# A hybrid decoder step on one core: sampled tokens' state space steps run in stages, the first norm ahead of the first weight, the residual behind the last head, convolution states beside z4 to z7

## The chip, the cores and the metric

The kernel runs on one core of a Trainium2 chip. Its time is the device time of one execution in microseconds (us); lower is better. A core has five engines with a queue each: TensorE (PE; PEld is its weight load), VectorE (DVE), ScalarE (ACT), GpSimd (POOL) and SyncE (SP). SP issues nearly all DMAs of this kernel, in order, from one queue. Every engine executes its own instructions in order; semaphores order them across engines.

## The reference

One layer of a decoder for 1024 prompt positions and 8 sampled tokens (1032 columns together, `NT`). After an RMSNorm one projection `w_in` feeds two mixers, and their outputs, each normed and gated, go through `w_out` and are added to the input; a gated MLP with a short convolution follows.

```python
h = rmsnorm(x, w['norm1_w'])
proj = h @ w['w_in']
q_r, f_r, i_r, g_r, z, xbc_r, dt_r = jnp.split(proj, splits, axis=-1)
...
o_a, S_h_new = hgrn2_mix(heads(q), heads(k), heads(i_r), heads(log_f), S_h)      # 8 heads
o_a = rmsnorm(o_a, w['hgrn_norm_w']) * jax.nn.silu(heads(g_r))
...
xbc, buf_s_new = causal_dwconv(xbc_r, buf_s, w['ssm_conv_w'], w['ssm_conv_b'])
xs, Bm, Cm = jnp.split(jax.nn.silu(xbc), [D_SSM, D_SSM + SSM_GROUPS * SSM_STATE], axis=-1)
y, S_s_new = ssd_scan(X * dt[..., None], A * dt, Bh, Ch, S_s)                    # 16 heads, 2 groups
y = (y + w['ssm_d'][:, None] * X).reshape(Bsz, L, D_SSM) * jax.nn.silu(z)
y = rmsnorm(y.reshape(Bsz, L, SSM_GROUPS, -1), ...)
...
x = x + jnp.concatenate([o_a, y], axis=-1) @ w['w_out']
```

For a sampled token the scan is one step: its state (64 x 128 per head, read from and written to memory) is decayed, gets `x * dt` times `B` added, and is multiplied by `C` and summed. This is the decode step below. New convolution states are outputs as well.

## The kernel before

Activations lie transposed: 128 features on the partitions, 1032 columns. Each fp32 product is made of three TensorE products of halves, high by high, low by high and high by low (`hh`, `hl` for activations; `wh`, `wl` for weights, rounded on ScalarE at L190 and subtracted on VectorE at L192). A projection job (`x0`, `z4`, `q3` ...) loads 512 KB of `w_in` and runs 3 chunks of 344 columns, 24 matmuls each, and evicts each chunk.

The order of the work on TensorE is written by hand. The list `jobs` holds the projections in order: the convolved inputs, z0 to z3, f, q, v, sg of head 0, z4 to z7, those of head 1 and on, and then `o8.0`, `o8.2`, `o12.0`, `o12.2`, `o8.4`, `o8.6`, `o12.4`, `o12.6` (the half of `w_out` for state space outputs, two blocks of 128 output rows each), and later the other half, the up and the down projection. `drive` runs the matmuls of these jobs between those of a chain: the state space scan of group 0, that of group 1, and the heads one after another, so that TensorE has work while the chain waits for VectorE. Smaller pieces hang on the count of job matmuls: `after(n, work)` runs `work` n of them later, and `spread` runs a generator's pieces so far apart. On the other engines a scheduler places the instructions by the order of issue and by the buffers, and it may draw an instruction ahead.

A decode step, `ssm_decode(g, i)`, treats 128 rows (two heads) for all 8 tokens in two halves of four tokens. Each half fetches the state `Sd` (256 KB) and the broadcast `Bb` and `Cb` (256 KB each), scales `Sd` on ScalarE in four instructions (L641), multiplies `Bb` (L642) and adds it (L643) on VectorE, stores the state, multiplies by `Cb` on GpSimd (L645) and reduces on VectorE (L646). It runs whole where it is called: group 0 at x5, x7, z0 and z1, beside the first scan, group 1 at z4 to z7. Its result goes into the 8 sampled columns of the same tile as the prompt's, and the gate and the norm (`ssm_gate`) work on all 1032 columns.

In a scan, `ssd_front` makes `bg`, `bt`, `xp`, `xdt` and the decays `csb`, `ssd_back` the products `yo`, `st`, `yd`, the new state `S` (L583) and the sums in `ecs` and `xbc`; `sT` transposes the last `S`. In a head, `vd` and `vtp` transpose v, `a` is the intra-chunk product, `ktp`, `kt` and `kv` make the chunk states, `o` the output, `dms` and `hms` the sums for its norm. Transposes to be done now and then (`vd`, `dms`, the convolution states' `cst`, the residual's `xtd`) share a PSUM tag, "nx", with a single buffer.

The residual: `token_blocks` copies the prompt in blocks to `xb_d`; `residual_load` fetches two 256 KB tiles `xs` for each of the eight row blocks m, and `residual` transposes them on VectorE in 32 x 32 blocks (L806), adds them on GpSimd (L803), and adds the sampled columns from a TensorE transpose `xtd` (L810, L811). It hangs on the o8 jobs; `o8.0` and `o8.2` run beside the last head.

At the start `first_norm` norms three tiles of 128 tokens (L112 to L118), then transposes them (`tp`) into `hh` and `hl`; the first two weights are loaded and rounded before.

Of the kernel before, what the change touches and what calls it, by code (L numbers as in the profile page):

```python
# [12 lines left out]
ALU = mybir.AluOpType  # L13
# [37 lines left out]
def hybrid_layer(  # L51
# [54 lines left out]
    def first_norm(tiles):  # L106
        xs = []
        for i in tiles:
            xt, t0, n = xtm[i]
            xn = [half("xn"), half("xn")]  # L110
            ss = keep.tile([P, 4], F32, tag="ss", bufs=4, name=nm("ss"))
            for i in range(2):  # L112
                A.activation(xn[i][:n], xt[:n, i * 512:(i + 1) * 512], AF.Square, accum_out=ss[:n, i:i + 1])
            V.tensor_tensor(ss[:n, 2:3], ss[:n, 0:1], ss[:n, 1:2], op=ALU.add)
            A.activation(ss[:n, 3:4], ss[:n, 2:3], AF.Sqrt, bias=epsc[:n], scale=1.0 / DM)
            V.reciprocal(ss[:n, 3:4], ss[:n, 3:4])
            for i in range(2):
                V.tensor_scalar(xn[i][:n], xt[:n, i * 512:(i + 1) * 512], ss[:n, 3:4], None, op0=ALU.mult)  # L118
            xs.append((xn, t0, n))
        c0, c1 = xs[0][1], xs[-1][1] + xs[-1][2]  # L120
        for k in range(KT):
            tp = bank("tp")
            for xn, t0, n in xs:
                PE.transpose(tp[:, t0 - c0:t0 - c0 + n], xn[k // 4][:n, (k % 4) * P:(k % 4 + 1) * P], ident[:n, :n])
            A.activation(hT_hi[k][:, c0:c1], tp[:, :c1 - c0], AF.Copy, scale=col("n1", k))
            V.scalar_tensor_tensor(hT_lo[k][:, c0:c1], tp[:, :c1 - c0], col("n1", k),
                                   hT_hi[k][:, c0:c1].bitcast(F32), op0=ALU.mult, op1=ALU.subtract)
# [52 lines left out]
    def wload(src, kt, m=P, kept=None):  # L180
# [9 lines left out]
        A.copy(wh[:, :n], ws[:, :n])  # L190
        if not again:
            V.tensor_tensor(wl[:, :n], ws[:, :n], wh[:, :n].bitcast(F32), op=ALU.subtract)  # L192
        if kept is not None:
            if again:
                SP.dma_start(wl.bitcast(F32), wl_d[kept[0]])
            else:
                SP.dma_start(wl_d[kept[0]], wl.bitcast(F32))
        return (wh[:, :n].rearrange("p (k m) -> p k m", m=m), wl[:, :n].rearrange("p (k m) -> p k m", m=m))
# [163 lines left out]

    def xbc_close(j, ext):
# [5 lines left out]
        A.activation(acc[:, :T], acc[:, :T], AF.Silu)  # L369
        A.activation(acc[:, T:NT], acc[:, T + 3:T + 32:4], AF.Silu)  # L370
# [21 lines left out]
    first = [(j, wload(w_in_[0, :, OFF_X + j * P:OFF_X + (j + 1) * P], KT), xbc_open()) for j in (8, 10)]  # L392
    for i in range(3, 9):
        load_x(i)
    vec_cols(0)
    for c in range(NCH):
# [29 lines left out]
    G.memset(dtr[:, :NT], 0.0)  # L426
# [98 lines left out]
    for g in range(4):  # L525
        rows = slice(32 * g, 32 * g + 32)
        V.tensor_copy(mlow[rows], lowf[rows, :, rows])
        V.tensor_copy(eyec[rows], ident[rows, rows])
# [99 lines left out]
    def ssm_decode(g, i):  # L628
        j = g * 4 + i
        xdd = small.tile([P, 2, ND], F32, tag="xdd", name=nm("xdd"))  # L630
        xdec = Xg[g][i][:, T:NT]
        V.tensor_tensor(xdd[:, 0, :], xdec, ddb[:, 0, j, :], op=ALU.mult)
        for b0 in (0, 4):
            bs = slice(b0, b0 + 4)
            Bb, Cb = tl("d", "Bb")[:, :512], tl("d", "Cb")[:, :512]
            for t_, r in ((Bb, 2 * g), (Cb, 2 * g + 1)):
                fetch(t_, bc_d[r, bs].rearrange("b n -> (b n)").unsqueeze(0).to_broadcast([P, 512]))
            Sd = tl("ld", "Sd")
            fetch(d4(Sd), state_ssm[0, bs, 2 * j:2 * j + 2].rearrange("b h p n -> (h p) b n"))
            for b in range(4):  # L640
                A.activation(d4(Sd)[:, b, :], d4(Sd)[:, b, :], AF.Copy, scale=ddb[:, 1, j, b0 + b:b0 + b + 1])  # L641
            V.tensor_tensor(d4(Bb), d4(Bb), cb(xdd[:, 0, bs]), op=ALU.mult)  # L642
            V.tensor_tensor(Sd, Sd, Bb, op=ALU.add)  # L643
            SP.dma_start(ssm_sample[0, bs, 2 * j:2 * j + 2].rearrange("b h p n -> (h p) b n"), d4(Sd))
            G.tensor_tensor(Cb, Sd, Cb, op=ALU.mult)  # L645
            V.tensor_reduce(xdd[:, 1, bs], d4(Cb), axis=mybir.AxisListType.X, op=ALU.add)  # L646
        V.scalar_tensor_tensor(xdec, xdec, d_bc[:, j:j + 1], xdd[:, 1, :], op0=ALU.mult, op1=ALU.add)

    def rstd_of(dst, tmp, ps, n):
# [6 lines left out]
    gr_d = dram.tile([2, 4, QW], F32, name="gr_d")  # L656

    def ssm_gate(g):
        acc = []

        def z_job(i):
            j = g * 4 + i

            def begin():
                if i == 0:
                    acc.append(tl("g", "gacc"))
                if g:
                    ssm_decode(1, i)
                elif i < 2:
                    ssm_decode(0, i + 2)  # L670

            def evict(c, cs, ps):
                Y = Xg[g][i][:, cs]
                sz = tl("z", "sz")[:, :CH]
                A.activation(sz, ps, AF.Silu)
                V.tensor_tensor(Y, Y, sz, op=ALU.mult)
# [9 lines left out]
        def rstd():  # L686
            ps = bank("ms", "nx")
            for q in range(4):
                mm(ps[32 * q:32 * q + 32, :QW], ones[:, 0:32], acc[0][:, q * QW:(q + 1) * QW])
            nt = tl("z", "nt")  # L690
            rstd_of(nt[:, :QW], tl("z", "nt")[:, :QW], ps[:, :QW], 512)
            SP.dma_start(gr_d[g], nt[::32, :QW])
            after(36, rows)

        def rows():
            fetch(acc[0][:, :NT], gr_d[g].rearrange("a t -> (a t)").unsqueeze(0).to_broadcast([P, NT]))
            after(20, lambda: spread(tail(), 6))

        def tail():
            for i in range(4):  # L700
                j = g * 4 + i
                Y = Xg[g][i][:, :NT]
                V.scalar_tensor_tensor(Y, Y, col("sn", j), acc[0][:, :NT], op0=ALU.mult, op1=ALU.mult)
                SP.dma_start(mix_d[8 + j], Y)
# [63 lines left out]
    G.memset(am, 0.0)  # L768
# [3 lines left out]
    V.tensor_tensor(selod, ident[:, 0:ND], ident[:, 32:32 + ND], op=ALU.add)  # L772
# [9 lines left out]

    def token_blocks():
        for m in range(KT):
            for a in range(4):
# [3 lines left out]
                yield  # L789

    def residual_load(m):
        ms = slice(m * P, (m + 1) * P)
        xs = [tl("d", "xs")[:, :512] for _ in range(2)]
        xd = small.tile([ND, P], F32, tag="xd", name=nm("xd"))
        for i in range(2):
            fetch(xs[i], xb_d[m][:, i * 512:(i + 1) * 512])
        fetch(xd, x_sample[:, 0, ms])
        return xs, xd

    def residual(out, xs, xd):  # L800
# [4 lines left out]
        for i0 in range(2):  # L805
            V.transpose(xs[i0], xs[i0])  # L806
            if i0 == 0:
                add(out[0][:, 0:512], xs[0])
                ps = bank("xtd", "nx")
                PE.transpose(ps[:, :ND], xd, ident[:ND, :ND])  # L810
                V.tensor_tensor(out[1][:, 508:516], out[1][:, 508:516], ps[:, :ND], op=ALU.add)  # L811
# [7 lines left out]
    def head_in(h):  # L819
# [8 lines left out]
        for n, off, func in (("f", OFF_F, AF.Tanh), ("q", OFF_Q, AF.Silu), ("v", OFF_I, AF.Copy),  # L828
# [4 lines left out]
            def begin(n=n):  # L833
                t[n] = tl("e" if h == 0 and n == "f" else "big", n)
# [218 lines left out]
    def out_job(r0, m, halves=(0, 1), last=False):  # L1053
        def load():
            w = wload(w_out[0, r0 * P:(r0 + 4) * P, m * P:(m + 2) * P], 4, 2 * P,
                      kept=(r0 // 4 * 4 + m // 2, halves[0]) if len(halves) == 1 else None)
            return w, [residual_load(m + i) for i in range(2)] if r0 == 8 else None

        def run(loads):
# [4 lines left out]
            if res:  # L1064
# [4 lines left out]
            for i in range(2):  # L1069
                for hf in halves:  # L1070
                    for c in range(2):
# [4 lines left out]
                        if res:  # L1076
# [8 lines left out]
                if res:  # L1085
                    spread(residual([xh[hf][m + i] for hf in range(2)], *res[i]), 8)
# [432 lines left out]
```

## Time and profile before

| | |
|---|---|
| median of 3 runs | 1765.24 us (1763.6 to 1767.99) |
| the profiled execution | 1764.89 us, its span 1763.2 us |
| mean granted TensorE clock | 0.995 |
| busy: PE, DVE, ACT, POOL | 1709.8, 1097.8, 778.7, 478.8 us |
| DMA queue of SP | 197.68 MB, 37.0% of 16 engines' span |

A row of a timeline gives start and duration in us, engine, line, operation, output and inputs, shape and count, and in brackets how long the engine idled before it and what released it. A row of waits gives the waiting engine and line, the releaser, the total in us, how often, and the longest. In a row of the windows the length of the window comes first, then busy us (and number of instructions) by engine, then the granted clock of TensorE (1.00 is full speed), the DMA share and GB/s.

### The profile page before, as it was taken

The page shows a single profiled execution, that of the slowest core. Times are in us where ns is not written, and L with a number is a line of the kernel's source. Part 1 is how long each engine was busy: PE and PEld are TensorE (multiplying, and loading weights), DVE is VectorE, ACT ScalarE, POOL GpSimd, SP SyncE. Part 2 cuts the span into 40 slices and gives each one's busy share as a digit, 9 for nine tenths or more (in the row PEclk, how much of TensorE's full clock was granted, in tenths as well). Part 3 has the DMA queues.
Part 4 walks back from the last instruction along what each step waited for, and adds up shares of the span by engine and source line. Part 5 has one row for each costly group of instructions (what it writes and reads, how often), then busy time and mean ns, then how long its engine had stood idle before and what let it go on. Part 6 is the DMA issues. An engine that isn't in the chain of part 4 may idle for free. (4 is left out here: it accounts for less than half of the span.)

```text
span 1763.2 us, 38543 instructions
## 1 busy us (share of the span) xinstructions
PE 1709.8 (97%) x16115; PEld 1659.4 (94%) x16115; DVE 1097.8 (62%) x1978; ACT 778.7 (44%) x1422; POOL 478.8 (27%) x485
## 2 busy tenths in 40 slices
PE   7999899999999999999799999999999999999998
PEld 6998789899999999999799989999999999999997
DVE  6668966566554554566636687776667767445545
ACT  7577686444434344344423374343333434111114
POOL 2103231111110110111220355666666664000002
PEclk9999999999999999999999999999999999999999
DMA  5355644553232332234336832222222226422312
GB/s 166 65 148 149 173 120 143 167 169 120 83 93 57 98 87 72 77 110 144 114 115 210 250 123 73 73 85 82 88 73 73 79 82 214 153 83 78 98 61 97
DMA packets 250132, 200.23 MB, mean 114 GB/s; under 512 B 47252, under 2 KB 220870, under 8 KB 249942
## 3 DMA queue, kind: packets, MB, share of 16 engines
q1 hardware_dynamic: 249670, 197.68, 37.0%
q8 instruction: 126, 2.06, 0.5%
q14 instruction: 48, 0.39, 0.1%
q0 software_dynamic: 288, 0.10, 0.0%
HBM read 155.17 MB, written 46.95 MB: 115 GB/s over the span
## 5 line engine op out<-in xcount | busy, mean ns | idle before, releaser
L93 PE MATMUL mm<-hl,wh 128*128 128x344 f32 x1248 | 406.1, 326 | 0.0
L93 PE MATMUL mm<-hh,wh 128*128 128x344 f32 x1248 | 405.6, 326 | 0.0
L93 PE MATMUL mm<-hh,wl 128*128 128x344 f32 x1248 | 402.8, 323 | 0.8 <-issue 0.8
L93 PEld LDWEIGHTS mm<-hl,wh 128*128 128x128 f32 x1248 | 236.1, 189 | 4.8 <-issue 4.2
L93 PEld LDWEIGHTS mm<-hh,wh 128*128 128x128 f32 x1248 | 236.1, 189 | 4.2 <-issue 3.4
L93 PEld LDWEIGHTS mm<-hh,wl 128*128 128x128 f32 x1248 | 236.3, 189 | 1.4 <-issue 1.2
L190 ACT CAST wh<-ws 128x1024 fp32r<-128x1024 f32 x96 | 100.6, 1048 | 254.9 <-PE dn L93 134.9
L93 PE MATMUL ub<-uh,wh 128*128 128x258 f32 x704 | 199.5, 283 | 4.2 <-DVE fext L1332 2.7
L93 PE MATMUL ub<-uh,wl 128*128 128x258 f32 x704 | 198.7, 282 | 0.0
L93 PE MATMUL ub<-ul,wh 128*128 128x258 f32 x704 | 198.6, 282 | 0.0
L93 PE MATMUL dn<-ah,wh 128*128 128x256 f32 (+1 forms) x640 | 181.1, 283 | 2.0 <-DVE x L1449 2.0
L93 PE MATMUL dn<-al,wh 128*128 128x256 f32 (+1 forms) x640 | 180.6, 282 | 0.0
L93 PE MATMUL dn<-ah,wl 128*128 128x256 f32 (+1 forms) x640 | 180.1, 281 | 0.0
L192 DVE TENSOR_TENSOR wl<-ws,wh 128x1024 fp32r<-128x1024 f32 x88 | 108.8, 1236 | 78.5 <-ACT wh L190 77.7
L93 PE MATMUL ua<-uh,wh 128*128 128x258 f32 x528 | 149.3, 283 | 1.5 <-DVE val L1344 1.3
L93 PE MATMUL mm<-mh,wh 128*128 128x258 f32 x512 | 146.9, 287 | 3.0 <-ACT x L1077 1.8
L93 PE MATMUL ua<-ul,wh 128*128 128x258 f32 x528 | 149.1, 282 | 0.0
L93 PE MATMUL ua<-uh,wl 128*128 128x258 f32 x528 | 148.4, 281 | 0.0
L93 PE MATMUL mm<-ml,wh 128*128 128x258 f32 x512 | 145.4, 284 | 0.9 <-DVE ml L1037 0.9
L93 PE MATMUL mm<-mh,wl 128*128 128x258 f32 x512 | 145.2, 284 | 0.0
L93 PEld LDWEIGHTS ub<-uh,wh 128*128 128x128 f32 x704 | 133.0, 189 | 4.9 <-DVE fext L1332 2.9
L1282 DVE TENSOR_TENSOR wl<-wt,wh 128x512 fp32r<-128x512 f32 x88 | 89.1, 1031 | 73.8 <-ACT wh L1281 73.8
(353 smaller groups left out, 3981.9 us busy)
## 6 DMA issues: line engine op xcount, KB each, us to landing
ws<-in_w_in_dram SPq DMA_DIRECT2D x52, 512.0 KB
ws<-in_w_up_dram SPq DMA_DIRECT2D x44, 512.0 KB
ws<-in_w_out_dram SPq DMA_DIRECT2D x24, 512.0 KB
act_d<-val SPq DMA_DIRECT2D x22, 516.0 KB
al<-act_d SPq DMA_DIRECT2D x22, 516.0 KB
ws<-in_w_down_dram SPq DMA_DIRECT2D x22, 512.0 KB
ml<-mix_d SPq DMA_DIRECT2D x48, 172.0 KB
csb<-cs_d SPq DMA_DIRECT2D x32, 256.0 KB
```

The source lines that it names most:

```text
L93: PE.matmul(out, lhsT, rhs, start=start, stop=stop)
L190: A.copy(wh[:, :n], ws[:, :n])
L192: V.tensor_tensor(wl[:, :n], ws[:, :n], wh[:, :n].bitcast(F32), op=ALU.subtract)
L1282: V.tensor_tensor(lo[:, cs], sums[name], hi[:, cs].bitcast(F32), op=ALU.subtract)
```

## The change

- *Start.* `wload` can hold back the rounding of a weight. The first weight's is issued behind the third tile's norm, the second's behind the first `hh` and `hl`; two GpSimd memsets and some small copies on VectorE wait until the third norm is done.
- *Decode steps.* Each is split into stages hung on the job count: fetches at once, the products of the first half 36 matmuls later, of the second 56, the first sum 64, the second 84. Group 0 starts at sg of head 0 and at z4, z5, z6, group 1 at v of heads 2 to 5 (that is, while the chains of heads 1 to 4 run). The sampled columns get tiles of their own, `xdk` and `szd`, and a gate and a norm of their own, with a sum on TensorE, `dgs`, in the "nx" bank. The prompt's norm covers 1024 columns.
- *Convolution states* move from beside heads 1 to 3 to z4 to z7, a piece each 24 matmuls instead of 60, and the token blocks follow 260 matmuls after.
- *Residual.* Blocks 0 to 3 go with `o8.4` and `o8.6`, 4 to 7 with `o12.4` and `o12.6`, none with `o8.0` and `o8.2`. The sampled tokens are transposed once, eight transposes in one bank copied to `xsT`.

```diff
+    def first_rounded():
+        with tc.issue_after(early[0].ins), tc.issue_after(early[1].ins):
+            held[0]()
+        behind.append(early[0].ins)
...
-        first_norm(range(3 * c, 3 * c + 3))
+        first_norm(range(3 * c, 3 * c + 3), *((None, None) if c else (first_rounded, held[1])))
...
-            if j in (5, 7):
-                ssm_decode(0, (5, 7).index(j))
...
-        xdec = Xg[g][i][:, T:NT]
+        xdec = xdk[:, j, :]
...
+        def front(bs, Bb, Cb, Sd):
             for b in range(4):
-                A.activation(d4(Sd)[:, b, :], d4(Sd)[:, b, :], AF.Copy, scale=ddb[:, 1, j, b0 + b:b0 + b + 1])
+                A.activation(d4(Sd)[:, b, :], d4(Sd)[:, b, :], AF.Copy, scale=ddb[:, 1, j, bs.start + b:bs.start + b + 1])
             V.tensor_tensor(d4(Bb), d4(Bb), cb(xdd[:, 0, bs]), op=ALU.mult)
             V.tensor_tensor(Sd, Sd, Bb, op=ALU.add)
...
+        after(36, lambda: front(*got[0]))
+        after(56, lambda: front(*got[1]))
+        after(64, lambda: back(*got[0]))
+        after(84, end)
...
+    def decode_norm(g, js, dg):
+        ps = bank("dgs", "nx")
+        mm(ps[:, :ND], ones, dg[:, 4, :])
+        rstd_of(dg[:, 4, :], dg[:, 5, :], ps[:, :ND], 512)
...
-                if g:
-                    ssm_decode(1, i)
-                elif i < 2:
-                    ssm_decode(0, i + 2)
+                if g and i < 3:
+                    ssm_decode(0, i + 1)
...
+            if m == 0:
+                ps = bank("xtd", "nx")
+                for k in range(KT):
+                    PE.transpose(ps[:, k * ND:(k + 1) * ND], xs[k // 4][:ND, blk[k % 4]], ident[:ND, :ND])
+                V.tensor_copy(xsT, ps[:, :KT * ND].rearrange("p (k b) -> p k b", b=ND))
...
-                ps = bank("xtd", "nx")
-                PE.transpose(ps[:, :ND], xd, ident[:ND, :ND])
-                V.tensor_tensor(out[1][:, 508:516], out[1][:, 508:516], ps[:, :ND], op=ALU.add)
+                add(out[1][:, 508:516], xsT[:, m, :])
...
+                if h == 0 and n == "sg":
+                    ssm_decode(0, 0)
+                elif 2 <= h <= 5 and n == "v":
+                    ssm_decode(1, h - 2)
...
-            return w, [residual_load(m + i) for i in range(2)] if r0 == 8 else None
+            rm = {(8, 4): 0, (8, 6): 2, (12, 4): 4, (12, 6): 6}.get((r0, m))
+            return w, [(rm + i, residual_load(rm + i)) for i in range(2)] if rm is not None else []
...
+    job("conv", None, once(lambda: spread(conv_states(), 24, lambda: after(260, lambda: spread(token_blocks(), 30)))))
     ssm_gate(1)
     heads[1] = head_in(1)
-    job("conv", None, once(lambda: spread(conv_states(), 60, lambda: spread(token_blocks(), 40))))
```

How the instructions move, at three places. First VectorE's queue in the first scan, around the state `S` of its third chunk. Before (`Sd`, `Cb` and `xdd` belong to a decode step, the rest to the scan):

```order
L643 TENSOR_TENSOR Sd_1696<-Sd_1696,Bb_1692 128x512 [waits Activation_49]
L552 TENSOR_TENSOR bt_1591<-bg_1588,tri 128x128 [waits Activation_49]
L560 TENSOR_TENSOR csb_1574<-csb_1574,bt_1591 128x512 [waits DVE_49]
L560 TENSOR_TENSOR csb_1580<-csb_1580,bt_1591 128x512
L646 TENSOR_REDUCE xdd_1690<-Cb_1693 128x4 [waits Pool_49]
L583 TENSOR_TENSOR S_1642<-S_1642,st_1640 128x512 [waits PE_49,Pool_49]
L643 TENSOR_TENSOR Sd_1711<-Sd_1711,Bb_1707 128x512 [waits DMAHW2_49,Activation_49]
L577 TENSOR_TENSOR ecs_1631<-yo_1634,ecs_1631 128x512 [waits DMAHW7_49,DMAHW6_49]
L646 TENSOR_REDUCE xdd_1690<-Cb_1708 128x4 [waits Pool_49]
```

And after, at the same place (`S`, `ecs`, `bt` are lines 611, 605 and 580 now):

```order
L624 SCALAR_TENSOR_TENSOR xbc_1187<-xbc_1187,d_bc,ecs_1523 128x128
L611 TENSOR_TENSOR S_1645<-S_1645,st_1643 128x512 [waits PE_49,Pool_49]
L605 TENSOR_TENSOR ecs_1634<-yo_1637,ecs_1634 128x512 [waits DMAHW2_49,DMAHW1_49]
L580 TENSOR_TENSOR bt_1594<-bg_1591,tri 128x128 [waits Activation_49]
L621 TENSOR_TENSOR ecs_1634<-yd_1648,ecs_1634 128x512 [waits DVE_49,PE_49]
```

The four decode instructions are gone from there, and `S` stands ahead of `bt` and `csb`. Second, VectorE's queue at the end of the second scan, around its last `S`. Before:

```order
L642 TENSOR_TENSOR Bb_3604<-Bb_3604,xdd_3602 128x512 [waits DMAHW5_49]
L577 TENSOR_TENSOR ecs_3461<-yo_3464,ecs_3461 128x512 [waits DMAHW3_49,DMAHW2_49,PE_49]
L642 TENSOR_TENSOR Bb_3619<-Bb_3619,xdd_3602 128x512 [waits DMAHW0_49]
L583 TENSOR_TENSOR S_3472<-S_3472,st_3470 128x512 [waits PE_49,Pool_49]
L593 TENSOR_TENSOR ecs_3461<-yd_3475,ecs_3461 128x512 [waits DVE_49,PE_49]
```

After:

```order
L674 TENSOR_TENSOR Bb_3399<-Bb_3399,xdd_3391 128x512 [waits DMAHW6_49]
L680 TENSOR_REDUCE xdd_3391<-Cb_3394 128x4 [waits Pool_49]
L675 TENSOR_TENSOR Sd_3401<-Sd_3401,Bb_3399 128x512 [waits DMAHW3_49,DVE_49,Activation_49]
L674 TENSOR_TENSOR Bb_3510<-Bb_3510,xdd_3508 128x512 [waits DMAHW4_49]
L605 TENSOR_TENSOR ecs_3336<-yo_3339,ecs_3336 128x512 [waits DMAHW1_49,DMAHW0_49,PE_49]
L611 TENSOR_TENSOR S_3347<-S_3347,st_3345 128x512 [waits PE_49]
```

Here it is now the steps (0,0) and (0,1) that stand ahead of `S`, with a reduction and a sum among them. Third, TensorE where the chain of head 0 begins. Before:

```order
L93 MATMUL mm_4079<-hl_96,wh_3852 128x344
L93 MATMUL mm_4079<-hh_88,wl_3853 128x344
L847 MATMUL vd_4109<-ident,v_3367 8x128
L852 MATMUL vtp_4113<-ident,v_3367 128x128 [waits PE_49]
L852 MATMUL vtp_4113<-ident,v_3367 128x128 x3
```

After:

```order
L93 MATMUL mm_4035<-hl_96,wh_3814 128x344
L93 MATMUL dgs_4059<-dg_4009,ones 128x8 [waits DVE_49]
L93 MATMUL mm_4035<-hh_88,wl_3815 128x344
L920 MATMUL vd_4077<-ident,v_3242 8x128 [waits DVE_49]
L925 MATMUL vtp_4081<-ident,v_3242 128x128 x4
```

`dgs` is new, one matmul ahead of `vd`, and `vd` now waits for VectorE, which reads `dgs`. The same stands ahead of head 5.

More of the change, by code (lines that the diff above doesn't have):

```diff
@@ L104, in load_x, with first_norm @@
         xtm.append((xt, i * P, n))
-    def first_norm(tiles):
+    early = [None, None]
+    def first_norm(tiles, then=None, mid=None):
         xs = []
@@ L178, in hybrid_layer, with wload @@
     nkept = [0]
-    def wload(src, kt, m=P, kept=None):
+    def wload(src, kt, m=P, kept=None, hold=None):
         ws = wpool.tile([P, KT * P], F32, tag="ws", bufs=2, name=nm("ws"))
@@ L189, in wload, with rounded @@
         last_w[0] = SP.dma_start(ws[:, :n].rearrange("p (k m) -> p k m", m=m), src.rearrange("(k p) m -> p k m", p=P))
[L190 to L197, printed above, removed]
+        def rounded():
+            A.copy(wh[:, :n], ws[:, :n])
+            if not again:
+                V.tensor_tensor(wl[:, :n], ws[:, :n], wh[:, :n].bitcast(F32), op=ALU.subtract)
+            if kept is not None:
+                if again:
+                    SP.dma_start(wl.bitcast(F32), wl_d[kept[0]])
+                else:
+                    SP.dma_start(wl_d[kept[0]], wl.bitcast(F32))
+        if hold is None:
+            rounded()
+        else:
+            hold.append(rounded)
         return (wh[:, :n].rearrange("p (k m) -> p k m", m=m), wl[:, :n].rearrange("p (k m) -> p k m", m=m))
@@ L361, in xbc_evict @@
             V.tensor_copy(last11[:, j, :], ps[:, CH - 11:])
+    xdk = const.tile([P, 8, ND], F32, name="xdk")
+    szd = const.tile([P, 8, ND], F32, name="szd")
     def xbc_close(j, ext):
@@ L390, in ssm_in @@
             xbc_job(g * 4 + i, put_in(Xg[g], i))
-    first = [(j, wload(w_in_[0, :, OFF_X + j * P:OFF_X + (j + 1) * P], KT), xbc_open()) for j in (8, 10)]
+    held = []
+    first = [(j, wload(w_in_[0, :, OFF_X + j * P:OFF_X + (j + 1) * P], KT, hold=held), xbc_open()) for j in (8, 10)]
     for i in range(3, 9):
@@ L425, in hybrid_layer @@
     dtr = tl("g", "dtr")
-    G.memset(dtr[:, :NT], 0.0)
+    late(G.memset(dtr[:, :NT], 0.0))
     for c, cs in enumerate(chunks):
@@ L527, in hybrid_layer @@
         V.tensor_copy(mlow[rows], lowf[rows, :, rows])
-        V.tensor_copy(eyec[rows], ident[rows, rows])
+        with tc.issue_after(behind[0]):
+            V.tensor_copy(eyec[rows], ident[rows, rows])
     def ssd_front(g, c, parts):
@@ L767, in hybrid_layer @@
     am = const.tile([P, NC, P], F32, name="am")
-    G.memset(am, 0.0)
+    late(G.memset(am, 0.0))
     qb = const.tile([P, ND, 32], F32, name="qb")
@@ L771, in hybrid_layer @@
     selod = const.tile([P, ND], F32, name="selod")
-    V.tensor_tensor(selod, ident[:, 0:ND], ident[:, 32:32 + ND], op=ALU.add)
+    with tc.issue_after(behind[0]):
+        V.tensor_tensor(selod, ident[:, 0:ND], ident[:, 32:32 + ND], op=ALU.add)
     for g in (64, 96):
@@ L781, in hybrid_layer @@
     xb_d = dram.tile([KT, P, T], F32, name="xb_d")
+    xsT = const.tile([P, KT, ND], F32, name="xsT")
     def token_blocks():
+        xs = [half("xd"), half("xd")]
+        for i in range(2):
+            fetch(xs[i][:ND], x_sample[:, 0, i * 512:(i + 1) * 512])
         for m in range(KT):
@@ L789, in token_blocks, with residual @@
                 yield
+            if m == 0:
[3 more added lines that the diff above has]
+                V.tensor_copy(xsT, ps[:, :KT * ND].rearrange("p (k b) -> p k b", b=ND))
     def residual_load(m):
-        ms = slice(m * P, (m + 1) * P)
         xs = [tl("d", "xs")[:, :512] for _ in range(2)]
-        xd = small.tile([ND, P], F32, tag="xd", name=nm("xd"))
         for i in range(2):
             fetch(xs[i], xb_d[m][:, i * 512:(i + 1) * 512])
-        fetch(xd, x_sample[:, 0, ms])
-        return xs, xd
-    def residual(out, xs, xd):
+        return xs
+    def residual(m, xs):
+        out = [xh[hf][m] for hf in range(2)]
         def add(x_, y_):
@@ L1085, in run @@
                 if res:
-                    spread(residual([xh[hf][m + i] for hf in range(2)], *res[i]), 8)
+                    spread(residual(*res[i]), 8)
         job(f"o{r0}.{m}" + (f".{halves[0]}" if len(halves) == 1 else ""), load, run)
```

69 lines of the change are left out of this document (50 added, 19 removed).

## The prediction, made before the changed kernel was run

> **What bounds the kernel now.** I read the page first, then the windows of 50 us, then the waits of TensorE in the windows where it idles, and last the timeline around each of those waits.
>
> ```profile
> span 1763.2 us, 38543 instructions
> PE 1709.8 (97%) x16115; PEld 1659.4 (94%) x16115; DVE 1097.8 (62%) x1978; ACT 778.7 (44%) x1422; POOL 478.8 (27%) x485
> ```
>
> TensorE bounds the kernel: it is busy for 1709.8 of 1763.2 us, so 53.4 us are idle. The change takes no matmul of weight away. It can win only idle time, and the stretches in which TensorE runs at half its clock. The windows say where those are (the columns after the colon are the length, then busy us of PE, PEld, DVE, ACT, POOL, the granted clock, the DMA share and GB/s).
>
> ```profile
> core 0: us, PE busy (x) PEld busy (x) DVE busy (x) ACT busy (x) POOL busy (x), PEclk, DMA share, GB/s
> 0.00:50.00 50.00, 38.42 (x227) 34.29 (x227) 29.69 (x78) 34.54 (x83) 9.05 (x26) 1.00 0.52 148
> ...
> 150.00:200.00 50.00, 45.90 (x327) 41.30 (x323) 43.30 (x73) 34.72 (x73) 16.34 (x16) 1.00 0.68 181
> 200.00:250.00 50.00, 46.04 (x289) 42.82 (x290) 38.34 (x64) 38.08 (x80) 14.92 (x13) 0.93 0.58 148
> ...
> 300.00:350.00 50.00, 47.12 (x314) 43.77 (x313) 31.50 (x51) 20.44 (x46) 11.62 (x9) 0.97 0.59 184
> ...
> 800.00:850.00 50.00, 44.58 (x714) 42.59 (x715) 39.20 (x72) 26.36 (x54) 13.03 (x11) 1.00 0.60 179
> 850.00:900.00 50.00, 44.01 (x388) 42.67 (x383) 26.47 (x58) 14.08 (x29) 6.34 (x7) 0.97 0.22 70
> 900.00:950.00 50.00, 50.00 (x414) 49.39 (x413) 24.38 (x50) 18.44 (x37) 11.26 (x12) 1.00 0.55 168
> ```
>
> Three places matter: the start (11.6 us idle), the two state space scans between 150 and 350 us (4.1, 4.0 and 2.9 us idle), and the last head with its residual between 800 and 900 us (5.4 and 6.0 us). Where VectorE is fullest, 43.30 and 39.20 of 50 us, TensorE idles. The waits of TensorE in the scans, then in the last head:
>
> ```profile
> PE sT L608 <- DVE S L583: 2.5, 1, 2.5
> PE yo L93 <- DVE S L583: 2.3, 2, 2.0
> PE xp L555 <- ACT xbc L369: 2.0, 1, 2.0
> PE yd L93 <- DVE xdt L557: 1.5, 1, 1.5
> ...
> PE bg L548 <- DVE S L583: 1.3, 1, 1.3
> PE xp L555 <- DVE ecs L577: 1.2, 1, 1.2
> ```
> ```profile
> PE xtd L810 <- DVE odr L956: 4.5, 1, 4.5
> PE mm L93 <- ACT x L1077: 1.8, 1, 1.8
> PE odp L93 <- DVE x L811: 1.5, 1, 1.5
> PE a L93 <- issue: 1.5, 1, 1.5
> PE a L93 <- DVE v L886: 1.3, 1, 1.3
> ```
>
> In the scans it is nearly always VectorE that releases TensorE. The timeline shows what VectorE itself waited for: a decode step of a sampled token stood at the head of its queue and its DMA had not landed.
>
> ```profile
> 171.80 0.69 DVE L642 TENSOR_TENSOR Bb<-Bb,xdd 128x512 f32<-128x512 f32 x1 [2.83 <-DMA Bb<-bc_d]
> 172.41 0.68 DVE L557 TENSOR_TENSOR xdt<-xp,dt 128x512 f32<-128x512 f32 x1
> ...
> 173.15 1.09 PE L93 MATMUL yd<-csb,xdt 128*64 128x128 f32 x16 [1.49 <-DVE xdt L557]
> ```
>
> Behind several such gaps the clock falls. The second line below is the same form of work as the first, at half speed, and so is the third beside the `yd` row above.
>
> ```profile
> 170.63 1.02 PE L93 MATMUL st<-xde,bt 128*128 128x512 f32 x2
> ...
> 207.55 1.92 PE L93 MATMUL st<-xde,bt 128*128 128x512 f32 x2
> 209.40 1.81 PE L93 MATMUL yd<-csb,xdt 128*64 128x128 f32 x16
> ```
>
> One such dip costs (1.92 - 1.02) + (1.81 - 1.09) = 1.6 us. I count four: two in 200 to 250 us (clock 0.93, behind the 2.0 us gaps at `yo` and `xp`), one in 300 to 350 (0.97, behind `sT`) and one in 850 to 900 (0.97, behind `xtd`). Here the Trainium skill speaks against the change: its page "TensorE: Matmul & The Clock Gate", Part 1, lets the clock fall only after an idle window of about 3.4 us, so that of these gaps only the 4.5 us one would count. This trace disagrees, with dips behind 2.0 and 2.5 us, but not after every gap of that size:
>
> ```profile
> 1055.00:1060.00 5.00, 2.28 (x19) 2.06 (x18) 4.01 (x6) 3.29 (x7) 2.26 (x2) 1.00 0.00 0
> ```
>
> There TensorE idles 2.72 us and the clock stays at 1.00. So a gap of 2 us can bring a dip, and need not.
>
> **The change part by part.** All against the profiled execution, 1764.9 us, 0.35 below the median of 1765.24.
>
> *Start.* The third tile's norm moves ahead of the first weight's low part on VectorE.
>
> ```profile
> 12.07 1.22 DVE L192 TENSOR_TENSOR wl<-ws,wh 128x1024 fp32r<-128x1024 f32 x1
> ...
> 13.40 0.49 DVE L118 TENSOR_SCALAR xn<-xt,ss 128x512 f32<-128x512 f32 x1
> 13.95 1.12 PE L124 MATMUL tp<-ident,xn 128*128 128x128 f32 x4 [1.94 <-DVE xn L118]
> ```
>
> With the 1.22 us and five small copies behind it, `xn` comes some 1.9 us earlier, and that gap of 1.94 us closes. But the second weight's rounding now stands behind the first `hh` on ScalarE, and both low parts stand between the `hl` on VectorE, so part returns. Bounds 0 and -3 (the gap, and 1.1 us more if the memsets that move off GpSimd had slowed the two `xn` before). I take **-1.5**.
>
> *Decode out of the first scan.* Gone from VectorE, ScalarE and GpSimd there are all steps like the 2.83 us wait. Between `xdt` and the last `S` nothing is added in their place; the x blocks' copies to `xb_d` stay in the DMA queue, without the 1 MB of each half. `yd`, `bg` and `yo` were late through VectorE's queue: 1.5 + 1.3 + 2.0, and the dip behind `yo`, 1.6, are won whole: 6.4. The `xp` at ScalarE's SiLU (2.0, with a dip of 1.6) and the `xp` behind `ecs` (1.2) also had the convolution's own passes and table loads ahead of them, which stay; I take half, 2.4. Bounds -3.5 (`yd` and `yo` alone, no dip) and -11.1 (all of it), taken **-8.7**, since the order leaves none of the steps that were waited for.
>
> *The `sT` gap.* The step is written for sg0, but the order shows decode (0,0) whole and the first product of (0,1) drawn into the last two chunks of the second scan, with three `Bb` ahead of the last `S` where two stood.
>
> ```profile
> 326.25 0.69 DVE L642 TENSOR_TENSOR Bb<-Bb,xdd 128x512 f32<-128x512 f32 x1 [2.15 <-DMA Bb<-bc_d]
> ```
>
> So the 2.5 us and its dip stay. Bounds -4.1 (both gone) and +2.2 (a third `Bb` waits as long); taken **+0.5**.
>
> *Convolution states beside z4 to z7.* Their transposes use the one "nx" bank and one `csr` buffer, and each next piece waits for a VectorE copy that now has decode products (0,1) to (0,3) ahead of it. Bounds 0 and 4.3 (two pieces as late as the `Bb` above); **+1.5**.
>
> *The decode norm on TensorE.* `dgs` fills the single "nx" bank one matmul before `vd` of the next head wants it, twice. What is queued behind `vd` is the whole head and its projections. The nearest rows are the same form in the heads, `dms`:
>
> ```profile
> 440.33 0.29 PE L93 MATMUL dms<-od,ones 128*128 128x8 f32 x2
> ...
> 441.15 1.28 ACT L651 ACT_TABLE_LOAD   x1
> 442.45 0.27 ACT L651 ACTIVATE od<-dms,epsc 128x8 f32<-128x8 f32 x1
> ...
> 442.75 0.17 DVE L652 SCALAR_TENSOR_TENSOR od<-dms,od 128x8 f32<-128x8 f32 x1 [0.83 <-ACT od L651]
> ```
>
> From `dms` to the end of that read: 2.6 us, of which 1.28 are the table load and 0.5 ScalarE's earlier work. In the changed program ScalarE has nothing to evict between the last chunk but one and `dgs`, so the load may run ahead. Bounds 0.3 and 2.6 each; I take 0.8, twice: **+1.6**.
>
> *Decode of group 1 in heads 1 to 4.* Four scalings per half, 1.56 us, stand ahead of the `kt` copies on ScalarE, and `kv` follows these.
>
> ```profile
> L641 ACT ACTIVATE Sd<-Sd,ddb 128x128 f32<-128x128 f32 x64 | 20.5, 391 | 13.3 <-DMA Sd<-in_state_ssm_dram 13.2
> 327.81 1.28 ACT L641 ACTIVATE Sd<-Sd,ddb 128x128 f32<-128x128 f32 x4 [7.35 <-DMA Sd<-in_state_ssm_dram]
> 428.10 1.08 ACT L964 COPY kt<-ktp 128x512 f32<-128x512 f32 x2 [2.03 <-PE ktp L963]
> 430.87 1.95 PE L93 MATMUL kv<-vt,kt 128*128 128x128 f32 x16
> ```
>
> ScalarE idles 2.03 us ahead of `kt`, and `kt` is done 1.69 us before `kv` starts: 3.72 us of cover, so 3.72 - 1.56 = 2.16 us are left for a late `Sd`. Over the whole kernel ScalarE waited 13.2 us for 16 loads of `Sd`. Bounds 0 and 27 (below); if two heads in four wait 0.5, **+1.0**. SP's queue is in order too: each half's output waits there for VectorE's sum, with the next weight's 512 KB behind it; the weights are asked for two jobs ahead, which hides a few microseconds of that.
>
> *Residual out of the last head.* The `xtd` gap and its dip go (4.5 + 1.6), `odp` behind `x` L811 goes (1.5). The 1.8, 1.5 and 1.3 us lie where VectorE's transposes and the residual's loads, 16 of 256 KB, stand among the head's own steps; I take half, 2.3. Bounds -6.1 and -12.2; **-9.9**.
>
> *Residual beside o8.4 to o12.6.* In 900 to 950 us, where half of it already ran, VectorE is busy for 24.38 us and TensorE for all 50: **0**, at most 2.
>
> Sum: -1.5 - 8.7 + 0.5 + 1.5 + 1.6 + 1.0 - 9.9 = **-15.5**: 1749.4 against the profiled execution, 1749.7 against the median.
>
> **The rivals.** *Scalings hold up the heads* (0.10). Each `Sd` of group 1 is queued behind a 512 KB weight. If it lands as late as the 7.35 us above, `kv` waits 7.35 - 2.16 = 5.2 us, with a dip 6.8; four heads give 27, and the time is 1749.7 - 1.0 + 27.2 = 1776. It is slower than before from 4.1 us a head, that is a landing 6.3 us after ScalarE's turn, or 4.7 if the clock falls too. Against it: the mean wait is 0.8 a load.
>
> *The load only moves* (0.13). Decode, now denser from the second scan to z7, costs there what it cost before: `sT` +2.2 instead of +0.5, the convolution +4.3 instead of +1.5, `dgs` +5.2 instead of +1.6: 1749.7 + 1.7 + 2.8 + 3.6 = 1758; with the two halves taken in the first scan lost as well, 1760.
>
> *The residual disturbs the output projection* (0.06): four jobs each with the 1.8 us wait of `mm` for `x`: +7.2, 1757. Against it the full window at 900.
>
> *The dips are not the gaps' doing* (0.05). Then three dips, of which I took 1.6, 0.8 and 1.6, stay when the gaps go: 1749.7 + 4.0 = 1753.7. For it speaks the gap at 1058 without a dip; against it that every dip here follows a gap. By the rule of the Trainium skill's page above, only the dip behind `xtd` would go: 1752.1.
>
> **How the numbers follow.** The forecast has 0.66 and its time is 1749.7. Its own range from the bounds, which seldom fall all on one side, is 1743 to 1757. The other cases reach down to 1741 (the first scan and the last head won whole, 4.7 more, a start of -3, no cost of the convolution and the heads, 2.5) and up to 1776; cut where 2 in 10 remain outside, the range is 1741 to 1763. A measurement of this kernel can tell about 0.3%, 5.3 us, from no change: faster is below 1759.9. Faster: 0.65 + 0.05 + 0.05 and half of the load's move, 0.03, together 0.78; same 0.13 (the rest of that case, the forecast's upper tail, a mild form of the first rival); slower 0.09.
>
> **What would show it.** Right: between 160 and 230 us no gap of TensorE over 1 us, and the window 200 to 250 at clock 1.00; in the last head no `xtd`, no wait of `odp` for `x`, no dip. `sT` waits again for `S`, some 2 to 4 us. `vd` of the first and sixth head waits about a microsecond for VectorE. Wrong: `kv` waiting for `kt` in heads 1 to 4, or gaps in the first scan that ScalarE's table loads release.

## The result and the profile after

The changed kernel takes 1775.45 us (median of 6 runs, 1772.44 to 1780.7), the kernel before 1763.83 (6 runs): 1.0067 times as long, with a 95% interval of 1.0051 to 1.0084. That is 11.6 us slower, where 15.5 us faster were forecast. The profiled execution takes 1775.22 us.

The page of the changed kernel, first its span and its engines:

```profile
span 1773.5 us, 38575 instructions
PE 1712.4 (97%) x16119; PEld 1662.7 (94%) x16119; DVE 1090.4 (61%) x1991; ACT 783.0 (44%) x1428; POOL 482.8 (27%) x501
```

The work is nearly the same; the idle time of TensorE grew from 53.4 to 1773.5 - 1712.4 = 61.1 us, and more of its busy time is at a lower clock (0.991 on average, for 0.995). Both traces cut at the same instructions of TensorE (start times subtracted, in us; the last stretch ends with the end of its last instruction) show where:

| stretch | before | after | change |
|---|---|---|---|
| start, up to the first product of a projection | 15.1 | 12.4 | -2.7 |
| first scan, up to `sT` of group 0 | 197.8 | 189.4 | -8.4 |
| second scan, up to `sT` of group 1 | 117.0 | 115.6 | -1.4 |
| z4 to z7, up to `vd` of head 0 | 58.8 | 70.9 | +12.1 |
| heads, up to `vd` of the sixth | 309.6 | 324.6 | +15.0 |
| up to `vd` of the last head | 122.0 | 121.7 | -0.3 |
| last head, up to its `hms` | 59.5 | 52.5 | -7.0 |
| output projection, up to the MLP | 159.5 | 162.6 | +3.1 |
| the rest | 716.1 | 716.2 | +0.1 |

So the start, the two scans and the last head got shorter, by 19.5 us together, and z4 to z7, the heads and the output projection got 30.2 longer. The windows of the changed kernel (columns as before) show the same:

```profile
core 0: us, PE busy (x) PEld busy (x) DVE busy (x) ACT busy (x) POOL busy (x), PEclk, DMA share, GB/s
150.00:200.00 50.00, 50.00 (x365) 45.44 (x363) 40.73 (x69) 34.41 (x70) 12.99 (x13) 1.00 0.46 111
200.00:250.00 50.00, 50.00 (x342) 47.08 (x337) 30.19 (x55) 41.84 (x80) 13.69 (x15) 1.00 0.30 85
...
300.00:350.00 50.00, 41.22 (x261) 38.16 (x260) 33.82 (x56) 24.09 (x59) 13.24 (x11) 0.93 0.73 206
...
500.00:550.00 50.00, 47.60 (x712) 45.17 (x712) 27.09 (x48) 22.36 (x36) 6.27 (x4) 0.97 0.34 99
...
600.00:650.00 50.00, 48.52 (x609) 46.90 (x610) 26.85 (x56) 26.40 (x48) 2.57 (x2) 0.97 0.33 94
650.00:700.00 50.00, 46.46 (x581) 45.16 (x581) 27.07 (x50) 19.07 (x40) 8.38 (x6) 0.93 0.36 108
...
850.00:900.00 50.00, 44.91 (x526) 43.38 (x525) 34.58 (x70) 20.93 (x45) 8.10 (x12) 0.93 0.43 137
900.00:950.00 50.00, 47.56 (x390) 46.72 (x389) 24.67 (x40) 15.44 (x32) 14.11 (x17) 1.00 0.44 138
```

From 150 to 250 us TensorE is full at clock 1.00. From 300 to 350 it idles 8.8 us at 0.93, and each 0.03 of clock in a window is one dip of the forecast's size (1.6 us), so there are now about eight dips for four. VectorE is busy for only some 27 of 50 us in the heads, and yet the waits of TensorE name it:

```profile
PE a L93 <- DVE q L959: 6.5, 4, 2.0
...
PE vd L920 <- DVE dg L711: 5.1, 2, 2.5
PE a L93 <- issue: 4.6, 3, 2.6
PE mm L93 <- DVE x L1153: 4.5, 7, 1.1
PE l L777 <- DVE csr L779: 3.7, 1, 3.7
PE sT L636 <- DVE S L611: 3.5, 1, 3.5
...
PE mm L93 <- ACT x L1151: 2.5, 1, 2.5
```

Each is a place of its own. The first is the heads'; the timeline of head 4 (SP's queue, GpSimd, VectorE, TensorE):

```profile
653.94 3.61 SPq L941 DMA_DIRECT2D out_dram<-Sh  x2
655.31 0.68 DVE L674 TENSOR_TENSOR Bb<-Bb,xdd 128x512 f32<-128x512 f32 x1
655.44 1.69 POOL L940 TENSOR_TENSOR Sh<-Sh,vb 128x512 f32<-128x512 f32 x1
...
658.57 0.40 SPq L182 DMA_DIRECT2D Bb<-bc_d  x1
...
662.48 0.69 DVE L674 TENSOR_TENSOR Bb<-Bb,xdd 128x512 f32<-128x512 f32 x1 [6.49 <-issue]
...
664.02 0.69 DVE L959 TENSOR_TENSOR q<-q,tt 128x512 f32<-128x512 f32 x1
...
664.85 0.75 PE L93 MATMUL a<-q,f 128*32 128x32 f32 x64 [1.37 <-DVE q L959]
```

The product of the second half of a decode step (`Bb`, L674) stands at the head of VectorE's queue for 6.49 us. Its fetch is issued by SP only at 658.57, behind two stores of `Sh` whose data GpSimd finishes at 657.1, and the product starts 3.9 us after the fetch. Behind it in VectorE's queue stands the head's own scaling `q` (L959), and behind that the next intra-chunk product `a` on TensorE. The name "issue" in the bracket says only that the profile shows no releaser.

### The profile page after: what moved, and what is told of

The parts are those of the page before. It is cut to its first block, busy times and chain, and to the rows that moved or that the text cites. A ratio compares the mean times of both kernels' runs of the same rounds, so it can differ in the third digit from the quotient of the medians.

```text
span 1773.5 us, 38575 instructions
## 1 busy us (share of the span) xinstructions
PE 1712.4 (97%) x16119; PEld 1662.7 (94%) x16119; DVE 1090.4 (61%) x1991; ACT 783.0 (44%) x1428; POOL 482.8 (27%) x501
```

## The experiments

Three theories of the heads' 15 us were tried first. A: VectorE is held by the product that waits for its fetch. B: ScalarE's scalings hold up the head's copies (the prediction's first rival). C: VectorE has simply too much to do in the heads. The rest of the loss was put to single edits of the changed kernel.

**The product behind the scaling.** The product gets one more dependency: it waits for the last ScalarE scaling of its own half, so the scheduler places it behind the point at which `Sd`, the last transfer of the half, has landed (in head 4 of the changed kernel SP issues `Sd` at 679.84, 21 us behind the second `Bb`). In the heads the order on ScalarE and in SP's queue stays, and so does VectorE's work.

```diff
-                A.activation(d4(Sd)[:, b, :], ...)
-            V.tensor_tensor(d4(Bb), d4(Bb), cb(xdd[:, 0, bs]), op=ALU.mult)
+                scaled = A.activation(d4(Sd)[:, b, :], ...)
+            prod_ = V.tensor_tensor(d4(Bb), d4(Bb), cb(xdd[:, 0, bs]), op=ALU.mult)
+            tc.add_manual_dep(prod_.ins, scaled.ins.name, ...)
```

> The changed kernel, with one thing more: each decode step's product on Bb (L674) waits for the last of ScalarE's four scalings of the same half, so it can no longer stand at the head of VectorE's queue while its transfer is under way. Theory A (in heads 1 to 4 the second Bb of each step holds up VectorE's f and q products, which TensorE's a waits for): the stretch from the first to the fifth head's end loses about 4 x 4 = 16 us of its growth, no wait of a for DVE q L959 is left, and the whole time falls from 1775 to about 1760. Theory B (it is ScalarE's scalings ahead of kt that hold up the heads, as the first rival had it): the order on ScalarE is the same, so the heads stay as they are, 1775. Theory C (VectorE is simply too full there with six more instructions of 0.69 us): nothing is taken away, 1772 to 1776.

Measured: 1763.34 us (10 runs), 0.9991 of before (0.998 to 1.0002). The heads take 309.9 us for 324.6. The largest waits of TensorE in its trace, but for one at the start:

```profile
PE vd L922 <- DVE dg L713: 5.1, 2, 2.5
PE mm L93 <- DVE x L1155: 4.1, 6, 1.1
PE sT L636 <- DVE S L611: 4.0, 1, 4.0
PE a L93 <- issue: 3.0, 1, 3.0
```

The wait of `a` for `q` is gone, by an edit that leaves ScalarE's order in the heads and the amount of VectorE's work alone: theory A, and B and C fall. VectorE still waits there, now for `Sd` by way of ScalarE's scalings (13.9 us in five waits, at most 3.8), but with the head's own steps ahead of the product in the queue:

```profile
672.10 0.69 DVE L674 TENSOR_TENSOR Bb<-Bb,xdd 128x512 f32<-128x512 f32 x1 [3.77 <-ACT Sd L673]
673.69 0.69 DVE L674 TENSOR_TENSOR Bb<-Bb,xdd 128x512 f32<-128x512 f32 x1
```

**The decode norm's sum in another bank**: `bank("dgs")` for `bank("dgs", "nx")`.

```diff
-        ps = bank("dgs", "nx")
+        ps = bank("dgs")
```

> The changed kernel with dgs in one of the four general PSUM buffers in place of the single nx buffer that vd takes next. Theory A (vd waits for VectorE to read dgs out of the one buffer, behind a weight's rounding and a table load on ScalarE): both gaps of 2.5 us at vd go, and the whole falls by about 5 us, to 1770. Rival: the waits move to the next user of the general buffers or to the eviction behind the table loads on ScalarE, and the whole falls by less than 2 us.

Measured: 1771.47 us (6 runs), 1.0041 (1.0026 to 1.0055). Both `vd` waits, 2.5 us each, are gone from the trace; the ratio is 0.26% lower than the changed kernel's, 4.6 us, though the two intervals overlap a little. In the one trace z4 to z7 is 2.3 us shorter, the heads, whose end held the other wait, only 0.8. What held the bank so long stands in the timeline of the changed kernel:

```profile
385.21 0.28 PE L93 MATMUL dgs<-dg,ones 128*128 128x8 f32 x2
...
385.41 1.04 ACT L199 CAST wh<-ws 128x1024 fp32r<-128x1024 f32 x1 [2.09 <-PE mm L93]
386.47 1.28 ACT L710 ACT_TABLE_LOAD   x1
387.76 0.27 ACT L710 ACTIVATE dg<-dgs,epsc 128x8 f32<-128x8 f32 x1
...
388.06 0.17 DVE L711 SCALAR_TENSOR_TENSOR dg<-dgs,dg 128x8 f32<-128x8 f32 x1 [0.35 <-ACT dg L710]
...
388.29 0.27 PE L920 MATMUL vd<-ident,v 128*8 128x128 f32 x1 [2.53 <-DVE dg L711]
```

ScalarE did idle ahead of `dgs`, 2.09 us, but at the head of its queue stood the rounding of a weight, which waited for TensorE to finish with that buffer at the end of the very same chunk. The table load came behind that.

**The convolution states back**: the job behind `heads[1]`, a piece each 60 matmuls, as in the kernel before; the rest as changed.

```diff
-    job("conv", None, once(lambda: spread(conv_states(), 24, lambda: after(260, lambda: spread(token_blocks(), 30)))))
...
+    job("conv", None, once(lambda: spread(conv_states(), 60, lambda: spread(token_blocks(), 40))))
```

> The changed kernel with the convolution states and the token blocks back behind head 1's projections, spread as before. Theory A (the second piece's transpose waits 3.65 us for a copy of csr that stands behind a decode reduction on VectorE, and a dip of the clock follows): the stretch from sT of group 1 to the first vd shrinks by 3 us of moved transposes and 5 us of waits; the heads take the 3 us back, so the whole falls by about 5 us, to 1770. Rival (the heads, which already wait for the decode steps, wait longer with the pieces beside them): the whole stays at 1773 to 1777.

Measured: 1773.34 us (4 runs), 1.0055 (1.0035 to 1.0074), which by itself can't be told from the changed kernel. The stretch z4 to z7 is 8.1 us shorter, the heads 6.2 longer:

```profile
PE a L93 <- DVE q L959: 7.6, 4, 2.4
```

The heads, already late through theory A, have the pieces as well. The piece that cost most in the changed kernel:

```profile
338.29 1.26 POOL L677 TENSOR_TENSOR Cb<-Sd,Cb 128x512 f32<-128x512 f32 x1 [3.01 <-DVE Sd L675]
339.58 0.69 DVE L680 TENSOR_REDUCE xdd<-Cb 128x4 f32<-128x512 f32 x1 [1.43 <-POOL Cb L677]
340.19 0.67 DVE L779 COPY csr<-l 11x512 f32<-11x512 f32 x1
...
340.91 1.02 PE L777 MATMUL l<-ident,last 128*11 128x128 f32 x4 [3.65 <-DVE csr L779]
```

The next transposes `l` need the bank that the copy `csr` empties; the copy stands in VectorE's queue behind a decode step's reduction, and this waits for GpSimd's product.

**The residual's places back**: all eight blocks with the o8 jobs, the sampled tokens still transposed once.

```diff
-            rm = {(8, 4): 0, (8, 6): 2, (12, 4): 4, (12, 6): 6}.get((r0, m))
+            rm = {(8, 0): 0, (8, 2): 2, (8, 4): 4, (8, 6): 6}.get((r0, m))
```

> The changed kernel with the residual's row blocks back at o8.0, o8.2, o8.4 and o8.6 (two each, half of them beside the last head), the sampled columns still from xsT. Theory A (the residual's transposes and loads beside the last head cost it 7 us, and beside o12.4 and o12.6 its GpSimd adds cost the output projection 3 us): the last head grows by about 5 to 7 us, the output stretch shrinks by 3, the whole is slower by 2 to 4 us, 1778. Rival (what cost the last head before was the xtd transpose on the nx bank alone, which is gone either way): the last head stays as it is and the output stretch shrinks by 3, 1772.

Measured: 1775.73 us (5 runs), 1.0063 (1.004 to 1.0085), which can't be told from the changed kernel. The last head gets only 1.4 us longer, the output projection 4.5 shorter, and z4 to z7, which the edit does not touch, 3.0 longer in that trace. The window of the output projection is full again, as before:

```profile
900.00:950.00 50.00, 50.00 (x421) 50.00 (x420) 22.43 (x42) 15.44 (x32) 12.66 (x16) 1.00 0.44 141
```

So moving the blocks lost 4.5 us in the output projection; that it won anything in the last head is not shown, since the last head takes 50.8 to 53.9 us in the first three experiments, which leave it alone. Most of its 7.0 us must then come from transposing the sampled tokens once instead of eight times through the shared bank, the other edit there. This is argued: no run put the eight transposes back.

**The kernel before with the same dependency.** If a waiting product also made its first scan slow, then the cure would work there without any move.

```diff
-                A.activation(d4(Sd)[:, b, :], ...)
-            V.tensor_tensor(d4(Bb), d4(Bb), cb(xdd[:, 0, bs]), op=ALU.mult)
+                scaled = A.activation(d4(Sd)[:, b, :], ...)
+            prod_ = V.tensor_tensor(d4(Bb), d4(Bb), cb(xdd[:, 0, bs]), op=ALU.mult)
+            tc.add_manual_dep(prod_.ins, scaled.ins.name, ...)
```

> The kernel before, with the one edit that helped the heads: each decode step's product on Bb waits for ScalarE's scalings of the same half. Theory A (the gaps of the two scans come from products that wait for a transfer at the head of VectorE's queue, not from the work itself): the gap at yd goes and the gaps behind it shrink, the first scan gets 4 to 7 us shorter with its decode steps still in it, the sT gap of 2.5 us goes, and the whole falls by 5 to 10 us, to 1755 to 1760. Rival (VectorE is too full there, 43 of 50 us, and only taking the steps out of the scan helps): the scans stay within 2 us, the whole at 1763 to 1766.

Measured: 1759.51 us (10 runs), 0.9983 (0.9973 to 0.9992), 2.8 us less than the 1762.29 of the kernel before beside it, where theory A expected 5 to 10. The first scan is 3.7 us shorter (`yd` still waits 1.3 us), the second 4.4, but z4 to z7 is 3.6 longer: there the scaling itself waits for its transfer, on ScalarE, ahead of an eviction that TensorE needs, and TensorE has two such waits for `sz`, 4.4 us together, that it did not have.

```profile
352.33 1.28 ACT L641 ACTIVATE Sd<-Sd,ddb 128x128 f32<-128x128 f32 x4 [3.08 <-DMA Sd<-in_state_ssm_dram]
...
354.45 0.45 ACT L677 ACTIVATE sz<-mm 128x344 f32<-128x344 f32 x1
...
354.95 0.43 PE L93 MATMUL mm<-hh,wh 128*128 128x344 f32 x1 [2.16 <-ACT sz L677]
```

**Three edits together, then two more.** First the dependency, the other bank and the convolution states back, in the changed kernel. Then, in addition, group 0's decode at z4 to z7, its products issued behind the last `S` of the second scan, against the wait of `sT`. Then the residual's places back as well.

```diff
-                if g and i < 3:
-                    ssm_decode(0, i + 1)
+                if g:
+                    ssm_decode(0, i)
...
-                if h == 0 and n == "sg":
-                    ssm_decode(0, 0)
...
+            with tc.issue_after(lastS[0].ins):
+                prod_ = V.tensor_tensor(d4(Bb), d4(Bb), cb(xdd[:, 0, bs]), op=ALU.mult)
```

> The changed kernel with the three mends together: product behind the scalings, dgs in another bank, convolution states back behind head 1. If their waits are separate, the gains add: 1763.3 less 4 (dgs, as measured) less 4 to 6 (convolution: 2 measured, but there the heads were crowded), 1753 to 1756. If they share one cause, the sum stays near 1760.

> As the three together, and group 0's decode steps begin at z4 to z7 instead of at sg of head 0 and z4 to z6, their products behind the last state of the second scan on VectorE. Theory: the sT gap of 3.5 to 4 us and the dip behind it go, 4 to 5 us less than the three together, about 1750. Rival: the fourth step, now partly under head 0, holds up its a or kv by as much, and the time stays as it is.

> As the one before, and the residual's row blocks back at o8.0 to o8.6. As measured alone, the last head grows by 1 to 2 us and the output stretch shrinks by 4: 2 to 3 us less than the one before, about 1747. Rival: beside a last head that is not late for other reasons the transposes cost the 7 us that they seemed to cost before, and it is 3 us slower than the one before.

Measured, against a kernel before at 1762.29 us: 1746.65 (0.9914, 0.9899 to 0.9929), 1746.47 (0.9919, 0.99 to 0.9938) and 1742.22 us (0.9888, 0.987 to 0.9905), 4 runs each. Against the changed kernel's ratio the single edits gave 0.76, 0.26 and 0.12% (1.0067 less 0.9991, 1.0041 and 1.0055), 1.14 together; the three at once give 1.53. With intervals of 0.1 to 0.2 to either side of each ratio that difference is not settled. The convolution states back cost the heads little once the product stands behind the scaling: z4 to z7 takes 59.0 us, and the heads, with the pieces in them and without the `vd` wait, 309.9, as in the first experiment the other way round. The second step trades one wait for another: `sT` no longer waits and the second scan is 2.7 us shorter, z4 to z7 is 1.7 longer, and no difference in time can be told. The third repeats the fourth experiment: the output projection is 3.7 us shorter, the last head 1.2 longer, within what it varies by. The intervals of the second step and the third overlap, so the size of this last gain is not settled. The last kernel has the lowest time of all that ran; it beats the kernel before by 1.1%. Its page and the largest waits of TensorE, but for one at the start:

```profile
span 1738.4 us, 38597 instructions
PE 1702.8 (98%) x16119; PEld 1655.0 (95%) x16119; DVE 1095.0 (63%) x1991; ACT 783.4 (45%) x1428; POOL 486.2 (28%) x501
```

```profile
PE tp L128 <- DVE xn L120: 3.5, 3, 2.1
PE mm L93 <- ACT sz L739: 2.9, 3, 1.2
PE ub L93 <- DVE fext L1409: 2.7, 1, 2.7
...
PE mm L93 <- ACT x L1154: 1.9, 1, 1.9
...
PE mm L93 <- DVE x L1156: 1.7, 3, 0.8
```

The one window up to 1700 us in which its clock is not 1.00:

```profile
800.00:850.00 50.00, 45.62 (x745) 43.79 (x744) 43.14 (x74) 26.91 (x60) 20.33 (x20) 0.93 0.55 170
```

With the same number of matmuls as the changed kernel TensorE is busy 9.6 us less, with two dips left of about eight, and idle for 35.6 us instead of 61.1. What remains is the start, the short waits at `sz`, the eviction `x` in the last head and a place in the MLP.

## Why the prediction was wrong

*Start*: right in kind, larger than forecast. -2.7 us at the first product of a projection, for -1.5 within bounds of 0 and -3.

*Decode out of the first scan*: right. -8.4 us for -8.7 (its own terms, 6.4 and 2.4, add up to 8.8). No gap over 1 us is left from 160 to 230 us and the clock of 200 to 250 is 1.00, as asked; a gap of 1.5 us at `xp`, at 115 us, is new. The experiment on the kernel before adds that 3.7 us of this stretch could be had without moving anything.

*The `sT` gap*: right that it stays. 3.5 us for 2.5; the stretch as a whole is 1.4 shorter. The dip that was to stay with it did not come: from 313 to 330 us the granted clock is 1.00.

*Decode of group 1 in heads 1 to 4*: **the step that failed**. Forecast +1.0, measured +15.0. One of the two `vd` waits, 2.5, is in that, and 3.0 us of the convolution pieces' matmuls have left the stretch, so that the steps cost it some 15. This is about half of the miss: 13.2 of the 26 us between the sum of the forecast and the change in the traces, with 9.8 in z4 to z7. I asked whether the decode's scalings on ScalarE leave room ahead of `kt`, and they do: `kt` was not late. I did not ask what its products bring to VectorE's queue, since by busy time they fit (0.69 us each). What they bring is a wait for a transfer. The rows of the kernel before had it in them: one `Bb` that waited 2.83 us was the very row by which I explained the first scan. I took that as the price of the scan's place, when it was the price of the order in the queue, and went with the step to its new place. The first rival's time, 1776, was nearly met by a mechanism that the rival did not have: it priced a late transfer in ScalarE's queue, the traces show one in VectorE's, and the first experiment tells the two apart. That its time came near is chance.

*Decode norm*: +0.8 taken for each `vd`, 2.5 measured, close to the upper bound of 2.6. I let the table load run ahead of `dgs` because ScalarE had nothing to evict; the weight's rounding stood there. The second experiment gives 4.6 us for both by the ratios.

*Convolution states*: +1.5 taken. The stretch grew by 12.1 us, of which some 3.0 are the pieces' own matmuls, which only came over from the heads, and one `vd` wait of 2.5; the 3.65 us gap behind `csr` and the dip behind it, two of the usual length in one (granted clock 0.57 from 339 to 347 us), are most of the rest. That my upper end of 4.3 was itself too low is borne out by the 8.1 us that the third experiment took out of the stretch, 3.0 of them the pieces' own.

*Residual out of the last head*: right in direction, -7.0 for -9.9. The waits at `xtd` and `odp` are gone, but the dip is not: the window at 850 us shows 0.93 for 0.97, two dips for one. Nor did the waits shrink that were put down to the residual's transposes and loads in the head's queues, for 2.3: that of a product for an eviction `x` grew from 1.8 to 2.5 us and that of `a` behind it from 1.5 to 2.6. Of the 16 loads that the prediction put there, the trace of the kernel before has eight beside the last head.

*Residual beside o8.4 to o12.6*: 0 taken, at most 2; +3.1 measured, and 4.5 back by the fourth experiment. I argued from VectorE's share of busy time. What TensorE waits for there is VectorE's eviction `x` (L1153, 4.5 us in seven waits, for 1.3 in three with the blocks back). Ahead of it in VectorE's queue stand the residual's transposes and the split of the loaded columns, and this is slower beside the residual's adds on GpSimd. Two rows of the split in the changed kernel, and GpSimd's add:

```profile
935.42 1.28 POOL L874 TENSOR_TENSOR x<-x,xs 128x508 f32<-128x508 f32 x1
935.46 1.62 DVE L1110 TENSOR_TENSOR ml<-ml,mh 128x344 fp32r<-128x344 f32 x1 [0.34 <-ACT mh L1109]
...
937.96 0.47 DVE L1110 TENSOR_TENSOR ml<-ml,mh 128x344 fp32r<-128x344 f32 x1
```

The same subtraction takes 0.47 us alone and 1.62 beside the add. The Trainium skill has this in kind: "GPSIMD Engine Reference", section "Specifications", says that GpSimd shares its memory interfaces with VectorE and that the two contend where VectorE's instruction has two inputs in SBUF. The rows agree. That this alone makes the 3.1 us was not isolated by a run.

Left open: why the second fetch stands behind the stores in SP's queue, and whether its buffer would have been free any sooner. The trace names only the stores: SP waits 8.0 us for the two `Sh` in head 4, and issues the second half's fetch 1 us after the later one without another wait. A run with buffers of its own for each half was not made.

## What to carry to other kernels

A step that waits for a transfer brings that wait into every in-order queue in which one of its instructions stands: before moving it, ask for each engine what is queued behind it at the new place, and first try to place its instructions behind the arrival of its last input, which was worth 0.76%, 13 us, in the changed kernel, where the whole move was to bring 15, and 0.17% in the kernel before. Free busy time on an engine does not hide a wait, and a buffer with a single copy can cost its next user the whole chain of reads, table load and foreign work included (here 2.5 us, twice). A move judged by itself can look useless while another wait covers its gain: the convolution states back were worth 2 us alone, and by estimate some 9 beside the other two edits (1.53 less 0.76 and 0.26 is 0.51%), though no run has those two without them.

## What the runs showed of the hardware

The clock of TensorE falls behind shorter gaps than I had reckoned with: in the changed kernel the windows at 500 and 600 us, whose longest waits are 1.7 and 2.0 us at `a`, show 0.97, and the window at 650, with 1.5 and 1.4 us, shows 0.93. The gap of 2.7 us at `ub` in the last kernel brings no dip, and neither does the one of 3.5 us at `sT` in the changed kernel; the same gap at `ub`, as long, brings one in the kernel with the three edits (0.97 from 1000 to 1050 us, for 1.00 in the last). So length alone does not decide, and what does is not settled. By the rule that the prediction cited, from the Trainium skill's page "TensorE: Matmul & The Clock Gate", Part 1, an idle window of about 3.4 us is needed; these dips disagree. A VectorE subtraction of two tiles in SBUF took 3.4 times as long (1.62 for 0.47 us) beside one add on GpSimd.
